# Prompt attention on one core: float32 probabilities as the stationary operand, V as the moving one

## The chip, the cores and the metric

The kernel runs on one core of a Trainium2 chip. The metric is device time in microseconds (us). A run of three timings of the kernel before gave a median of 1132.84 us (1131.6 to 1136.12).

The engines are named as the profile names them: PE (TensorE, matmuls) with PEld (its weight loads: the operand that is loaded is the stationary one, the other streams past it and is the moving one), DVE (VectorE), ACT (ScalarE), POOL (GpSimd) and SP (SyncE, which here only issues DMAs).

## The reference

One decoder layer for a prompt of 1024 tokens and 8 sample tokens: a projection, an attention group (8 heads of 64, 2 key/value heads) with three branches, a recurrent group (HGRN2), and an output stage. The change touches the prompt's attention alone. Cut to that:

```
qg = q / sqrt(64)
# three branches: compressed blocks (c), selected blocks (s), window of 512 (w)
s_x = einsum(qg, k_x) - slope * distance
p_x = softmax(s_x under its mask)
o_x = einsum(p_x, v_x)
o   = g[...,0:1]*o_c + g[...,1:2]*o_s + g[...,2:3]*o_w
```

All of it is float32.

## The kernel before, in words

The program is one static order of instructions for each engine. A scheduler makes that order when the program is built, from the order in which the code is written and from priorities. Each engine then works through its own list in order and waits at semaphores.

The stages follow one another: projection and recurrence, compression of the keys, the projections of the gates, attention, and the output stage (`finish`). The attention stage takes 16 units: 8 blocks of 128 queries times 2 key/value groups, in the order of blocks 5, 6, 7, 4, 3, 2, 1, 0. A unit (`branches`) does branch 2 (compressed keys, one block of at most 63 keys), then branch 0, then branch 1 (blocks of 128 keys each). In all there are 16 blocks of branch 2 and 132 of the other two.

For one block PE makes the scores of four heads at once (keys on partitions, 4 x 128 query columns) with two matmuls into a PSUM tile `ph` (two buffers): `ph<-QA,KA` and `ph<-QB,KB`. ACT takes the exponential into the tile `P` (float32). On some blocks POOL masks `P`. Then `P` is split into two parts that PE can multiply in one pass each (type `fp32r`): `Ph`, a rounded copy, and `Pl`, the rest `P - Ph`. Two blocks in three have the copy on ACT and the subtraction on POOL; every third has both on DVE. V is split ahead of the stage into `Vh` and `Vl`. PE then adds three products into the accumulator `pb` (two buffers), with the 65 columns of V (64 and a column of ones for the denominator) as the stationary operand and the 512 columns of probabilities as the moving one. Branch 2 packs its split parts into one tile `PH` and needs two products (`vcl`, `vch`).

When a branch is done (`output`), ACT copies the accumulator (65 x 512, queries along the free dimension) to `oT`; PE transposes four pieces of it into a tile `pa` (three buffers); DVE computes the factor `rden` (reciprocal of the denominator times the gate) and scales into `og` or `onrm`; POOL adds.

Around this other work is interleaved: `maxima`, which for the unit after next multiplies keys and queries (`pa<-KB,QB`) and takes row maxima on DVE (`junk`, `mx`), then turns them (`pa<-ident,Mp`) into a row of `QB`; and the attention of the 8 sample tokens (`sample_attention`: `sg`, `KT`, `Qr`, `PT`, `two` and others), one step after every second block. The helper `mm` issues all matmuls, so they have one line (L42); `split` has lines L50 and L51.

Of the kernel before, what the change touches and what calls it, by code (L numbers as in the profile page):

```python
# [7 lines left out]
F32 = mybir.dt.float32  # L8
F32R = mybir.dt.float32r
# [4 lines left out]
OP = mybir.AluOpType  # L14
# [6 lines left out]
NB = 8  # L21
# [6 lines left out]
class Kernel:  # L28
# [766 lines left out]
    def prompt_setup(self, ctx):  # L795
        nc, a, ap = self.nc, self.a, self.kvpool
# [11 lines left out]
        for br in range(3):  # L808
            for g in range(2):
                n = self.KA[br, g].shape[1]  # L810
                nc.sync.dma_start(self.KB[br, g][64:68].bitcast(F32), self.kx_d[br, :, :n])
        self.Vh = ap.tile([128, 2, 8, 2, 65], F32R, name="Vh")
        self.Vl = ap.tile([128, 2, 8, 2, 65], F32R, name="Vl")
        self.vch = ap.tile([128, 2, 65], F32R, name="vch")
        self.vcl = ap.tile([64, 2, 65], F32R, name="vcl")
        one = ap.tile([128, 2, 32], F32, name="one")
        for v, val in ((self.Vh, 1.0), (self.Vl, 0.0)):
            nc.gpsimd.memset(one[:, 0 if val else 1], val)
            nc.vector.tensor_copy(v[:, :, :, :, 64], one[:, 0 if val else 1].rearrange("p (a b c) -> p a b c", a=2, b=8))
        nc.vector.tensor_copy(self.vch, one[:, 1, :1, None].to_broadcast([128, 2, 65]))  # L820
        nc.vector.tensor_copy(self.vcl, one[:64, 1, :1, None].to_broadcast([64, 2, 65]))
        nc.vector.tensor_copy(self.vch[:, :, 64], one[:, 0, :2])
        for half in range(2):
            hs = slice(half * 512, half * 512 + 512)
            for br in range(2):
                rows = self.kv_d[1 + br][hs].rearrange("(i p) c -> p i c", p=128)
                k = stage()
                nc.sync.dma_start(k, rows[:, :, :128])
                pt = self.ps_h.tile([128, 512], F32, name="ph")
                for i in range(4):  # L830
                    nc.tensor.transpose(pt[:, i * 128:(i + 1) * 128], k[:, i], self.ident)
                for g in range(2):
                    A, B = self.KA[br, g], self.KB[br, g]
                    src = pt[g * 64:g * 64 + 64]
                    here, there = (A[64:128, hs], B[0:64, hs])[::1 if g else -1]
                    nc.scalar.copy(here, src)
                    nc.sync.dma_start(there.bitcast(F32), here.bitcast(F32))
                    nc.vector.tensor_tensor(A[0:64, hs], src, here.bitcast(F32), op=OP.subtract)
                v = stage()
                nc.sync.dma_start(v, rows[:, :, 128:])  # L840
                sl = (slice(None), br, slice(4 * half, 4 * half + 4), slice(None), slice(0, 64))
                self.split(self.Vh[sl], self.Vl[sl], v.rearrange("p i (h d) -> p i h d", h=2), nc.scalar, nc.gpsimd)

        mask = ap.tile([128, 640], F32, name="mask")
        nc.gpsimd.memset(mask, 0.0)
# [10 lines left out]
        for g in range(2):  # L856
# [3 lines left out]
            nc.scalar.copy(B[0:64, :63], src)  # L860
            nc.scalar.copy(A[64:128, :63], src)
            nc.vector.tensor_tensor(A[0:64, :63], src, (A[64:128, :63] if g else B[0:64, :63]).bitcast(F32), op=OP.subtract)
        vc = self.vcS[:63, NB].rearrange("p (h d) -> p h d", h=2)
        nc.scalar.copy(self.vch[64:127, :, :64], vc)
        self.split(self.vch[:63, :, :64], self.vcl[:63, :, :64], vc, nc.scalar, nc.vector)
        self.zero = ap.tile([128, 4], F32, name="zero")
        nc.gpsimd.memset(self.zero, 0.0)
        self.PH = ap.tile([128, 4, 128], F32R, name="PH")
        self.filled = 64
        self.Mp, self.QB, self.QA, self.nblk = {}, {}, {}, 0  # L870
        for g in range(2):
            for i in range(2):
                Mp = self.Mp[g, i] = ap.tile([128, 4, 4], F32R, name=f"Mp{g}{i}")
# [76 lines left out]
    def branches(self, qb, g, i):  # L950

        nc, wk = self.nc, self.ap
        KA, KB, QA, QB = self.KA, self.KB, self.QA[g, i], self.QB[g, i]
        og = wk.tile([128, 4, 64], F32, name="og", bufs=3)
        for br in (2, 0, 1):
            k0, k1 = (0, 0) if br == 2 else self.ranges(qb)[br]
            acc = self.ps_b.tile([128, 512], F32, name="pb")[:65]
            for kb in range(k0, k1 + 1):
                def block(br=br, kb=kb, first=kb == k0, last=kb == k1, acc=acc):
                    n = 8 * qb + 7 if br == 2 else 128  # L960
                    ks = slice(kb * 128, kb * 128 + n)
                    ps = self.ps_h.tile([128, 512], F32, name="ph")[:n].rearrange("p (h q) -> p h q", q=128)
                    self.mm(ps, KA[br, g][:, ks], QA, True, False)
                    self.mm(ps, KB[br, g][:68, ks], QB, False, True)
                    P = wk.tile([128, 4, 128], F32, name="P", bufs=5)[:n]
                    nc.scalar.activation(P, ps, AF.Exp, scale=0.125)  # L966
                    keep = dict(compare_op=OP.is_ge, fill=0.0)
                    if br == 2:
                        nc.gpsimd.affine_select(P, P, pattern=[[0, 4], [1, 128]], base=qb * 128 - 31, channel_multiplier=-16, **keep)
                    elif kb == qb:  # L970
                        nc.gpsimd.affine_select(P, P, pattern=[[0, 4], [1, 128]], base=0, channel_multiplier=-1, **keep)
                    elif br == 1 and kb == qb - 4:
                        nc.gpsimd.affine_select(P, P, pattern=[[0, 4], [-1, 128]], base=0, channel_multiplier=1, **keep)
                    PH = self.PH if br == 2 else wk.tile([128, 4, 128], F32R, name="Ph", bufs=3)
                    if br == 2:
                        if self.filled > n:
                            nc.vector.tensor_copy(PH, self.zero[:, :, None].to_broadcast([128, 4, 128]))
                        self.filled = n
                    Ph = PH[:n]
                    Pl = PH[64:64 + n] if br == 2 else wk.tile([128, 4, 128], F32R, name="Pl", bufs=2)  # L980
                    self.nblk += 1
                    self.split(Ph, Pl, P, nc.scalar if self.nblk % 3 else nc.vector, nc.gpsimd if self.nblk % 3 else nc.vector)
                    if br == 2:
                        self.mm(acc, self.vcl[:n, g], Ph, True, False)
                        self.mm(acc, self.vch[:, g], PH, False, True)
                    else:
                        vh, vl = self.Vh[:, br, kb, g], self.Vl[:, br, kb, g]
                        self.mm(acc, vh, Ph, first, False)
                        self.mm(acc, vl, Ph, False, False)
                        self.mm(acc, vh, Pl, False, last)  # L990

                yield block

            def output(br=br, acc=acc):
                oT = wk.tile([128, 512], F32, name="oT", bufs=2)[:65]
                nc.scalar.copy(oT, acc)
                pt = self.ps_a.tile([128, 512], F32, name="pa").rearrange("p (h d) -> p h d", h=4)
                for hh in range(4):
                    nc.tensor.transpose(pt[:, hh, :65], oT[:, hh * 128:(hh + 1) * 128], self.ident[:65, :65])
                r = wk.tile([128, 4], F32, name="rden", bufs=2)  # L1000
                nc.vector.tensor_scalar(r, pt[:, :, 64], 1e-30, None, op0=OP.max)
                nc.vector.reciprocal(r, r)
                gi = 12 * g + (0 if br == 2 else 1 + br)
                nc.vector.tensor_tensor(r, r, self.G[:, qb, gi:12 * g + 12:3], op=OP.mult)  # L1004
                rb = r[:, :, None].to_broadcast([128, 4, 64])
                if br == 2:
                    nc.vector.tensor_tensor(og, pt[:, :, :64], rb, op=OP.mult)
                elif qb == 0:
                    for hh in range(4):
                        nc.vector.scalar_tensor_tensor(og[:, hh], pt[:, hh, :64], r[:, hh:hh + 1], og[:, hh], op0=OP.mult, op1=OP.add)  # L1010
                else:
                    t = wk.tile([128, 4, 64], F32, name="onrm", bufs=2)
                    nc.vector.tensor_tensor(t, pt[:, :, :64], rb, op=OP.mult)
                    nc.gpsimd.tensor_tensor(og, og, t, op=OP.add)

            yield output

        def store():
            nc.sync.dma_start(self.oa_d[qb * 128:qb * 128 + 128, g * 256:(g + 1) * 256], og.rearrange("p h d -> p (h d)"))

        yield store
# [397 lines left out]
```

## Time and profile before

| | |
|---|---|
| median of three timings | 1132.84 us |
| the profiled execution's own time | 1139.19 us |
| its span, first to last instruction | 1137.5 us |
| attention stage, read from the timeline | about 549 to 903 us |

The profiled execution is one run, 6.35 us above the median; 1.69 us of it lie outside its span. In the rows below, times are us unless marked ns. PE's busy time counts each matmul from its start to a modelled end, and matmuls overlap, so the step from one start to the next is what a matmul costs PE. The granted clock is the share of PE's full clock: 1.0 is 2.4 GHz, 0.5 is 1.2 GHz.

### The profile page before, as it was taken

The page shows a single profiled execution, that of the slowest core. Times are in us where ns is not written, and L with a number is a line of the kernel's source. Part 1 is how long each engine was busy: PE and PEld are TensorE (multiplying, and loading weights), DVE is VectorE, ACT ScalarE, POOL GpSimd, SP SyncE. Part 2 cuts the span into 40 slices and gives each one's busy share as a digit, 9 for nine tenths or more (in the row PEclk, how much of TensorE's full clock was granted, in tenths as well). Part 3 has the DMA queues.
Part 4 walks back from the last instruction along what each step waited for, and adds up shares of the span by engine and source line. Part 5 has one row for each costly group of instructions (what it writes and reads, how often), then busy time and mean ns, then how long its engine had stood idle before and what let it go on. Part 6 is the DMA issues. An engine that isn't in the chain of part 4 may idle for free.

```text
span 1137.5 us, 18238 instructions
## 1 busy us (share of the span) xinstructions
PE 1061.9 (93%) x6457; PEld 879.9 (77%) x6457; DVE 726.8 (64%) x1931; ACT 465.3 (41%) x939; POOL 391.2 (34%) x378
## 2 busy tenths in 40 slices
PE   4999999999899999999899898898888999999998
PEld 3998799999798998999576565665555688778876
DVE  6857564656655436436686989998999575372213
ACT  4622234223122345422376565656565442141112
POOL 0033233222211130021384665666677333122111
PEclk9999999999899999999798899998799699999999
DMA  6211203434545664215559020005331283131110
GB/s 203 59 32 61 66 13 108 132 103 131 161 145 168 186 211 162 74 61 157 187 163 258 19 56 19 20 19 148 112 94 38 61 244 113 40 102 47 47 42 30
DMA packets 116768, 116.41 MB, mean 102 GB/s; under 512 B 14614, under 2 KB 98926, under 8 KB 114372
## 3 DMA queue, kind: packets, MB, share of 16 engines
q1 hardware_dynamic: 95172, 79.46, 24.2%
q10 hardware_dynamic: 19200, 19.01, 4.9%
q0 software_dynamic: 2304, 16.78, 4.3%
q8 instruction: 51, 0.84, 0.3%
q14 instruction: 41, 0.34, 0.1%
HBM read 84.84 MB, written 29.31 MB: 100 GB/s over the span
## 4 chain that ended last, share of the span: by engine, by line
PE 70%; DVE 15%; DMA 7%; issue 4%; ACT 2%; POOL 1%; SPq 0%; DVEq 0%; ACTq 0%; POOLq 0%
PE pa L42 35%; PE pb L42 20%; PE ph L42 7%; PE pt L42 3%; DMA vb<-v_d 2%; DMA w_raw<-w_in 2%; DVE junk L927 2%; DVE Pl L51 2%; DVE KT L51 1%; PE ph L714 1%; DVE fw_lo L51 1%; DVE rden L1004 1%; DVE Ph L50 1%; DMA sg<-cache_slc_kv,pidx 1%; PE pa L1149 1%
## 5 line engine op out<-in xcount | busy, mean ns | idle before, releaser
L51 POOL TENSOR_TENSOR Pl<-P,Ph 128x512 fp32r<-128x512 f32 x87 | 123.4, 1423 | 59.1 <-PE pb L42 42.5
L42 PE MATMUL pa<-xhi,w_hi 128*128 128x344 f32 x384 | 125.6, 329 | 3.7 <-ACT w_hi L238 2.2
L42 PE MATMUL pa<-xlo,w_hi 128*128 128x344 f32 x384 | 124.1, 325 | 0.0
L42 PE MATMUL pa<-xhi,w_lo 128*128 128x344 f32 x384 | 123.3, 326 | 0.2 <-DVE w_lo L239 0.2
L966 ACT ACTIVATE P<-ph 128x512 f32<-128x512 f32 (+4 forms) x148 | 85.1, 592 | 47.7 <-PE ph L42 44.4
L42 PE MATMUL pa<-KB,QB 65*128 65x320 f32 (+6 forms) x195 | 68.2, 368 | 16.3 <-DVE mx L927 9.9
L927 DVE CUSTOM_DVE_ANT_0 junk<-pa,mask 128x320 bf16<-128x320 f32 (+5 forms) x150 | 72.4, 492 | 13.7 <-PE pa L42 12.5
L42 PE MATMUL pa<-w_lo,xhi 128*128 128x256 f32 (+2 forms) x256 | 79.6, 315 | 0.2 <-DVE w_lo L239 0.2
L238 ACT ACTIVATE w_hi<-w_raw,gpre 128x512 fp32r<-128x512 f32 (+2 forms) x80 | 47.3, 616 | 78.2 <-DMA w_raw<-w_in 45.5
L42 PE MATMUL pa<-w_hi,xlo 128*128 128x256 f32 (+2 forms) x256 | 79.3, 314 | 0.0
L42 PE MATMUL pa<-w_hi,xhi 128*128 128x256 f32 (+2 forms) x256 | 78.5, 316 | 0.0
L42 PEld LDWEIGHTS pa<-xhi,w_hi 128*128 128x128 f32 x384 | 73.3, 191 | 5.3 <-ACT w_hi L238 2.8
L42 PEld LDWEIGHTS pa<-xhi,w_lo 128*128 128x128 f32 x384 | 72.7, 190 | 0.6 <-DVE w_lo L239 0.4
L42 PEld LDWEIGHTS pa<-xlo,w_hi 128*128 128x128 f32 x384 | 73.0, 190 | 0.1
L42 PEld LDWEIGHTS pa<-KB,QB 65*128 65x128 f32 x195 | 39.3, 205 | 37.7 <-DVE mx L927 14.3
L42 PE MATMUL ph<-QA,KA 128*128 128x512 f32 (+4 forms) x148 | 66.2, 448 | 1.6 <-DVE mx L927 1.6
L556 POOL TENSOR_TENSOR K<-K,E 128x512 f32<-128x512 f32 x24 | 34.1, 1423 | 96.9 <-PE pb L42 59.9
L239 DVE SCALAR_TENSOR_TENSOR w_lo<-w_raw,gpre,w_hi 128x512 fp32r<-128x512 f32 (+2 forms) x80 | 52.1, 672 | 23.2 <-ACT w_hi L238 22.4
L42 PE MATMUL pb<-Pl,Vh 128*65 128x512 f32 x132 | 57.6, 436 | 5.5 <-DVE Pl L51 4.2
L42 PE MATMUL pa<-fw_hi,yh 128*128 128x512 f32 (+1 forms) x160 | 61.8, 386 | 0.2 <-ACT fw_hi L50 0.2
L42 PE MATMUL ph<-QB,KB 68*128 68x512 f32 (+4 forms) x148 | 61.3, 431 | 0.4 <-ACT QB L946 0.2
L42 PE MATMUL pa<-fw_hi,yl 128*128 128x512 f32 (+1 forms) x160 | 61.5, 384 | 0.0
(482 smaller groups left out, 2888.1 us busy)
## 6 DMA issues: line engine op xcount, KB each, us to landing
w_raw<-w_in SPq DMA_DIRECT2D x32, 256.0 KB
w_raw<-w_in SPq DMA_DIRECT2D x48, 128.0 KB
VS<-sg SPq DMA_DIRECT2D x8, 512.0 KB
sg<-cache_win_kv SPq DMA_DIRECT2D x16, 256.0 KB
fw_raw<-w_out SPq DMA_DIRECT2D x16, 256.0 KB
fw_raw<-ple_gate SPq DMA_DIRECT2D x16, 256.0 KB
f_x<-x_prompt SPq DMA_DIRECT2D x8, 512.0 KB
win_kv_sample<-cache_win_kv SPq DMA_DIRECT2D x8, 511.0 KB
```

Of the source, the lines that this page charges most:

```text
L42: return self.nc.tensor.matmul(out, lhsT, rhs, start=start, stop=stop, skip_group_check=True)
L50: (hi_eng.copy if hi_eng is self.nc.scalar else hi_eng.tensor_copy)(hi, src)
L51: lo_eng.tensor_tensor(lo, src, hi.bitcast(F32), op=OP.subtract)
L238: nc.scalar.activation(hi, raw, AF.Copy, scale=g)
L239: nc.vector.scalar_tensor_tensor(lo, raw, g, hi.bitcast(F32), op0=OP.mult, op1=OP.subtract)
L556: nc.gpsimd.tensor_tensor(Kv[:, :, 0], Kv[:, :, 0], Ev[:, :, 1:2].to_broadcast([128, nb, m]), op=OP.mult)
L714: nc.tensor.transpose(pt[:, i * 128:(i + 1) * 128], src[b0 + j // 2, kv][:, j % 2, 2 * jp:2 * jp + 2].rearrange("p j d -> p (j d)"), self. ...
L927: nc.vector.tensor_tensor_reduce(junk, pm, mk, 1.0, -1e30, op0=OP.add, op1=OP.max, accum_out=o)
L966: nc.scalar.activation(P, ps, AF.Exp, scale=0.125)
L1004: nc.vector.tensor_tensor(r, r, self.G[:, qb, gi:12 * g + 12:3], op=OP.mult)
L1149: nc.tensor.transpose(pt[:, j * 128:(j + 1) * 128], rows(j), self.ident)
```

## The change

The splits go. `P` itself, float32, is the stationary operand: for each head 128 key rows by 128 query columns. V, float32 too and not split, is the moving one with its 65 columns. One matmul in the code for each head and block adds into the accumulator, whose four heads now lie side by side with queries on partitions. So nothing is transposed when a branch is done: DVE reads the accumulator, keeps the denominator's reciprocal in a free column of it, and scales from it. V is loaded with 16 DMAs straight into its tile, where 4 DMAs and 4 splits stood.

```diff
-        self.Vh = ap.tile([128, 2, 8, 2, 65], F32R, name="Vh")
-        self.Vl = ap.tile([128, 2, 8, 2, 65], F32R, name="Vl")
...
+        self.V = ap.tile([128, 2, 8, 2, 65], F32, name="V32")
+        self.vc = ap.tile([64, 2, 65], F32, name="vc32")
+        nc.gpsimd.memset(self.V[:, :, :, :, 64], 1.0)
+        nc.gpsimd.memset(self.vc[:, :, 64], 1.0)
...
-                v = stage()
-                nc.sync.dma_start(v, rows[:, :, 128:])
-                sl = (slice(None), br, slice(4 * half, 4 * half + 4), slice(None), slice(0, 64))
-                self.split(self.Vh[sl], self.Vl[sl], v.rearrange("p i (h d) -> p i h d", h=2), nc.scalar, nc.gpsimd)
+                for i in range(4 * half, 4 * half + 4):
+                    nc.sync.dma_start(self.V[:, br, i, :, :64], self.kv_d[1 + br][i * 128:i * 128 + 128, 128:].rearrange("p (h d) -> p h d", h=2))
...
-            acc = self.ps_b.tile([128, 512], F32, name="pb")[:65]
+            acc = self.ps_b.tile([128, 512], F32, name="pb").rearrange("p (h d) -> p h d", h=4)
...
-                    self.split(Ph, Pl, P, nc.scalar if self.nblk % 3 else nc.vector, nc.gpsimd if self.nblk % 3 else nc.vector)
-                    if br == 2:
-                        self.mm(acc, self.vcl[:n, g], Ph, True, False)
-                        self.mm(acc, self.vch[:, g], PH, False, True)
-                    else:
-                        vh, vl = self.Vh[:, br, kb, g], self.Vl[:, br, kb, g]
-                        self.mm(acc, vh, Ph, first, False)
-                        self.mm(acc, vl, Ph, False, False)
-                        self.mm(acc, vh, Pl, False, last)
+                    v = self.vc[:n, g] if br == 2 else self.V[:, br, kb, g]
+                    for hh in range(4):
+                        m = self.mm(acc[:, hh, :65], P[:, hh], v, first and hh == 0, last)
...
             def output(br=br, acc=acc):
-                oT = wk.tile([128, 512], F32, name="oT", bufs=2)[:65]
-                nc.scalar.copy(oT, acc)
-                pt = self.ps_a.tile([128, 512], F32, name="pa").rearrange("p (h d) -> p h d", h=4)
-                for hh in range(4):
-                    nc.tensor.transpose(pt[:, hh, :65], oT[:, hh * 128:(hh + 1) * 128], self.ident[:65, :65])
+                pt = acc
...
+                nc.vector.tensor_scalar(pt[:, :, 66], pt[:, :, 64], 1e-30, None, op0=OP.max)
+                nc.vector.reciprocal(pt[:, :, 66], pt[:, :, 66])
+                nc.vector.tensor_tensor(r, pt[:, :, 66], self.G[:, qb, gi:12 * g + 12:3], op=OP.mult)
```

On PE, in branch 1 of the first unit, this stood in the order before (a row is line, operation, out<-in, shape of what is written, and a count where a row repeats; `sg` belongs to the sample tokens):

```order
L42 MATMUL pb<-Ph,Vh 65x512
L42 MATMUL pb<-Ph,Vl 65x512
L42 MATMUL pa<-KB_5360,QB_5494 128x448
L1149 MATMUL pa<-ident,sg 128x128 x4
L42 MATMUL pb<-Pl,Vh 65x512
L42 MATMUL ph<-QA,KA_5363 128x512
L42 MATMUL ph<-QB_5487,KB_5364 128x512
```

And this stands there now, two blocks further on in the same branch:

```order
L42 MATMUL pb<-V_5375,P 128x65 x3
L1121 MATMUL pa<-ident,sg 128x128 x8
L42 MATMUL pa<-KB_5360,QB_5481 128x448
L42 MATMUL pb<-V_5375,P 128x65
L42 MATMUL ph<-QA,KA_5363 128x512
L42 MATMUL ph<-QB_5474,KB_5364 128x512
L42 MATMUL pb<-V_5375,P 128x65 x4
```

The three wide products of a block have become four narrow ones, one for each head, and other work is set between them as before. At the entry to the stage, 7 products of `maxima` stood between the last matmul of the gate projection and the first scores; now 16 do.

On DVE, where the first branch of the first unit is put out, this stood before (L1001 to L1007 are the output; the rows around it are a split and the maxima):

```order
L1001 TENSOR_SCALAR rden<-pa 128x4
L1002 RECIPROCAL rden<-rden 128x4
L50 CAST Ph<-P 128x512
L1004 TENSOR_TENSOR rden<-rden,G 128x4
L1007 TENSOR_TENSOR og<-pa,rden 128x256
```

And this stands at the end of the first unit now, where two branches are put out at once (`KT` belongs to the sample tokens, L912 to the maxima, L974 to L985 are the output):

```order
L51 TENSOR_TENSOR KT_6383<-pa,KT_6382 128x512
L912 ISA junk,mx<-pa,mask 128x320
L912 ISA mx 128x1
L974 TENSOR_SCALAR pb<-pb 128x4 x2
L975 RECIPROCAL pb<-pb 128x4 x2
L976 TENSOR_TENSOR rden<-pb,G 128x4 x2
L985 TENSOR_TENSOR onrm<-pb,rden 128x256
```

DVE no longer splits, and its output reads `pb` itself, the accumulator, where it read a copy that PE had turned.

On ACT, in the first unit, this stood before:

```order
L50 CAST Ph<-P 128x512 x2
L966 ACTIVATE P<-ph 128x512 x2
L50 CAST Ph<-P 128x512
L50 CAST KT_6265<-pa 128x512
L996 COPY oT<-pb 65x512
```

And this stands there now:

```order
L951 ACTIVATE P<-ph 128x512 x2
L50 CAST KT_6238<-pa 128x512
L1152 COPY K_6196<-pa 128x512
L951 ACTIVATE P<-ph 128x512 x4
L50 CAST KT_6289<-pa 128x512
```

The copies into `Ph` and `oT` are gone; the exponentials follow one another more closely.

## Rows read from the trace of the kernel before

**Rows 1.** The page, part 1: busy us, share of the span, instructions.
```profile
PE 1061.9 (93%) x6457; PEld 879.9 (77%) x6457; DVE 726.8 (64%) x1931; ACT 465.3 (41%) x939; POOL 391.2 (34%) x378
```

**Rows 2.** Busy PE, PEld, DVE, ACT, POOL; clock, DMA, GB/s, by stretch.
```profile
549.00:903.00 354.00, 312.27 (x1570) 205.70 (x1571) 308.17 (x903) 216.72 (x398) 224.98 (x217) 0.89 0.32 92
...
650.00:700.00 50.00, 46.26 (x229) 31.47 (x228) 45.81 (x129) 31.39 (x61) 30.37 (x28) 0.98 0.15 40
```

**Rows 3.** The chain that ended last, in the attention stage: shares by line.
```profile
by line: PE pb L42 16.3%; PE ph L42 11.8%; issue 8.7%; PE pa L42 6.3%; DVE junk L927 5.7%; PE pt L42 5.1%; DVE Pl L51 5.1%; DVE KT L51 4.5%; DVE rden L1004 4.1%; DVE Ph L50 3.5%; DVE fw_lo L51 3.3%; DMA sg<-cache_slc_kv,pidx 3.2%; PE pa L11
```

**Rows 4.** PE's groups in the attention stage: shapes, count, busy, mean ns, idle before.
```profile
L42 PE MATMUL ph<-QA,KA 128*128 128x512 f32 (+4 forms) x148 | 66.2, 448 | 1.6 <-DVE mx L927 1.6
L42 PE MATMUL pa<-KB,QB 65*128 65x320 f32 (+6 forms) x176 | 62.3, 371 | 16.3 <-DVE mx L927 9.9 <-DVE mx L929 2.3 <-DVE rden L1002 1.0
...
L42 PE MATMUL pb<-Pl,Vh 128*65 128x512 f32 x131 | 57.2, 437 | 5.5 <-DVE Pl L51 4.2 <-POOL Pl L51 0.7 <-DVE rden L1004 0.3
...
L999 PE MATMUL pa<-ident,oT 65*128 65x65 f32 x184 | 22.4, 237 | 0.6 <-DVE mx L927 0.5
...
L42 PE MATMUL pt<-KT,PT 128*16 128x128 f32 x192 | 16.8, 230 | 1.1 <-DVE KT L51 1.1
```

**Rows 5.** Timeline of PE where it is packed: start, duration, what.
```profile
653.83 0.34 PE L42 MATMUL pa<-KB,QB 65*128 65x384 f32 x1
654.00 0.39 PE L42 MATMUL pb<-Pl,Vh 128*65 128x512 f32 x1
654.23 0.39 PE L42 MATMUL pb<-Ph,Vh 128*65 128x512 f32 x1
...
660.44 0.41 PE L999 MATMUL pa<-ident,oT 65*128 65x65 f32 x4
660.65 0.42 PE L42 MATMUL pa<-KB,QB 65*128 65x384 f32 x1
```

**Rows 6.** The tile `two`: count, least/median/most ns, first and last start, shape.
```profile
L42 PE MATMUL pt<-two,o x16: 251/251/272, 765.0 to 766.7; 16*128 16x8 f32 x16
```

**Rows 7.** Timeline of PE in the compression: float32 products with 63 stationary columns.
```profile
450.42 0.90 PE L42 MATMUL pt<-w,w1r 128*63 128x64 f32 x12
451.25 0.45 PE L42 MATMUL pb<-x,w1h 128*128 128x384 f32 x1
```

**Rows 8.** Groups of DVE, ACT and POOL in the attention stage.
```profile
L51 DVE TENSOR_TENSOR Pl<-P,Ph 128x512 fp32r<-128x512 f32 x45 | 39.9, 887 | 2.4 <-PE pb L42 2.1
L50 DVE CAST Ph<-P 128x512 fp32r<-128x512 f32 x45 | 34.7, 771 | 3.5 <-ACT P L966 1.9 <-PE pb L42 1.0 <-POOL P L971 0.7
L1004 DVE TENSOR_TENSOR rden<-rden,G 128x4 f32<-128x4 f32 x46 | 29.0, 630 | 0.5
...
L1013 DVE TENSOR_TENSOR onrm<-pa,rden 128x256 f32<-128x256 f32 x28 | 11.7, 419 | 0.4
...
L50 ACT CAST Ph<-P 128x512 fp32r<-128x512 f32 x87 | 53.2, 618 | 11.3 <-POOL Pl L51 3.8 <-PE pb L42 2.7 <-POOL P L971 2.1
L996 ACT COPY oT<-pb 65x512 f32<-65x512 f32 x47 | 27.1, 579 | 20.4 <-PE pb L42 16.1 <-PE pa L999 3.9
...
L51 POOL TENSOR_TENSOR Pl<-P,Ph 128x512 fp32r<-128x512 f32 x87 | 123.4, 1423 | 59.1 <-PE pb L42 42.5 <-ACT Ph L50 14.9 <-ACT P L966 1.0
...
L51 POOL TENSOR_TENSOR PH<-P,PH 47x512 fp32r<-47x512 f32 (+7 forms) x12 | 16.1, 1339 | 9.0 <-ACT PH L50 7.4 <-issue 1.3
```

**Rows 9.** The line L1004: least, median and most ns over the kernel.
```profile
L1004 DVE TENSOR_TENSOR rden<-rden,G x48: 147/560/1862, 574.8 to 910.5; 128x4 f32<-128x4 f32 x48
```

**Rows 10.** Timeline of DVE at the entry to the stage: the maxima's steps.
```profile
550.10 0.48 DVE L927 CUSTOM_DVE_ANT_0 junk<-pa,mask 128x320 bf16<-128x320 f32 x1
550.51 0.08 DVE L927 DVE_READ_ACCUMULATOR2_ANT mx<- 128x1 f32 x1
```

**Rows 11.** Timeline of SP (DMA issues) while keys and V are loaded.
```profile
500.52 0.50 SPq L828 DMA_DIRECT2D st<-kv_d  x1
505.92 0.36 SPq L840 DMA_DIRECT2D st<-kv_d  x1
```

More of the change, by code (lines that the diff above doesn't have):

```diff
@@ L811, in prompt_setup @@
                 nc.sync.dma_start(self.KB[br, g][64:68].bitcast(F32), self.kx_d[br, :, :n])
-        self.Vh = ap.tile([128, 2, 8, 2, 65], F32R, name="Vh")
-        self.Vl = ap.tile([128, 2, 8, 2, 65], F32R, name="Vl")
[L814 to L822, printed above, removed]
+        self.V = ap.tile([128, 2, 8, 2, 65], F32, name="V32")
+        self.vc = ap.tile([64, 2, 65], F32, name="vc32")
+        nc.gpsimd.memset(self.V[:, :, :, :, 64], 1.0)
+        nc.gpsimd.memset(self.vc[:, :, 64], 1.0)
         for half in range(2):
@@ L862, in prompt_setup @@
             nc.vector.tensor_tensor(A[0:64, :63], src, (A[64:128, :63] if g else B[0:64, :63]).bitcast(F32), op=OP.subtract)
[L863 to L870, printed above, removed]
+        nc.vector.tensor_copy(self.vc[:63, :, :64], self.vcS[:63, NB].rearrange("p (h d) -> p h d", h=2))
+        self.Mp, self.QB, self.QA = {}, {}, {}
         for g in range(2):
@@ L973, in block @@
                         nc.gpsimd.affine_select(P, P, pattern=[[0, 4], [-1, 128]], base=0, channel_multiplier=1, **keep)
-                    PH = self.PH if br == 2 else wk.tile([128, 4, 128], F32R, name="Ph", bufs=3)
-                    if br == 2:
[L976 to L980, printed above, removed]
@@ L981, in block @@
-                    self.nblk += 1
-                    self.split(Ph, Pl, P, nc.scalar if self.nblk % 3 else nc.vector, nc.gpsimd if self.nblk % 3 else nc.vector)
-                    if br == 2:
-                        self.mm(acc, self.vcl[:n, g], Ph, True, False)
-                        self.mm(acc, self.vch[:, g], PH, False, True)
-                    else:
-                        vh, vl = self.Vh[:, br, kb, g], self.Vl[:, br, kb, g]
-                        self.mm(acc, vh, Ph, first, False)
-                        self.mm(acc, vl, Ph, False, False)
-                        self.mm(acc, vh, Pl, False, last)
+                    v = self.vc[:n, g] if br == 2 else self.V[:, br, kb, g]
@@ L992, in branches @@
+                    for hh in range(4):
+                        m = self.mm(acc[:, hh, :65], P[:, hh], v, first and hh == 0, last)
+                        if first:
+                            if hh:
+                                self.after(m, start)
+                            else:
+                                start = m
                 yield block
             def output(br=br, acc=acc):
-                oT = wk.tile([128, 512], F32, name="oT", bufs=2)[:65]
-                nc.scalar.copy(oT, acc)
@@ L997, in output @@
-                pt = self.ps_a.tile([128, 512], F32, name="pa").rearrange("p (h d) -> p h d", h=4)
-                for hh in range(4):
-                    nc.tensor.transpose(pt[:, hh, :65], oT[:, hh * 128:(hh + 1) * 128], self.ident[:65, :65])
+                pt = acc
                 r = wk.tile([128, 4], F32, name="rden", bufs=2)
-                nc.vector.tensor_scalar(r, pt[:, :, 64], 1e-30, None, op0=OP.max)
-                nc.vector.reciprocal(r, r)
                 gi = 12 * g + (0 if br == 2 else 1 + br)
-                nc.vector.tensor_tensor(r, r, self.G[:, qb, gi:12 * g + 12:3], op=OP.mult)
+                nc.vector.tensor_scalar(pt[:, :, 66], pt[:, :, 64], 1e-30, None, op0=OP.max)
```

## The prediction

> **What bounds the kernel now.** I read the page's first part first. PE is busy 93% of the span and DVE 64% [rows 1]; that is an average over stages, and only the attention stage is changed. So I read the busy time by stretch there: of 354 us PE is busy 312, DVE 308, POOL 225, ACT 217, at a mean granted clock of 0.89 [rows 2]. Two engines look full. The reader should mistrust PE's figure, since a matmul's modelled time overlaps the next one's. The step from start to start is what it costs: in a packed piece of the timeline 0.23 us for 512 columns (654.00 to 654.23), 0.17 for 384, and 0.05 for each of the four transposes of an output (the next product starts 0.21 us after the first of them) [rows 5].
>
> With these steps PE's own work in the stage can be counted at the full clock. 148 blocks have two score products, 132 blocks three products with V, 16 blocks (branch 2) two, and the sample tokens have 48 of the same width: 772 products of 512 columns at 0.23 us, 178 us. Add 176 products of the maxima at about 0.16 us, 28 us, and some 530 small ones, of which 184 turn outputs and 192 are the sample tokens' [rows 4], at 0.05 to 0.1 us, 35 us. That is about 240 us of 354. The other 114 us are waits and stretches at 1.2 GHz; a mean clock of 0.89 over 354 us alone stands for up to 39 us.
>
> The chain of waits says on whom PE waits. It runs in turn over PE (the four lines shown sum to 39.5%) and DVE: the maxima's line L927 5.7%, the split's `Pl` 5.1% and `Ph` 3.5%, `rden` 4.1%, `KT` 4.5% [rows 3]. So the stage is bound by two engines that hand work to each other, both with little slack.
>
> **What the change costs on PE.** Before, a block of branches 0 and 1 cost three steps of 0.23, 0.69 us. Now it has four float32 products, each with 128 stationary columns and 65 moving ones. The trace of before has no such product, but it has close neighbours. The records show that a float32 product is two records: the code makes 8 products into `two`'s output and the trace has 16 [rows 6]. Those have 128 stationary columns and only 8 moving ones, and yet 15 steps take 1.7 us, 0.113 us each [rows 6], so it is not the moving columns that set the pace there. Products with 63 stationary and 64 moving columns take at most 0.069 us a record (0.83 us for 12) [rows 7]. The lower bound for a new product is therefore 2 x 0.069, the upper one 2 x 0.113 = 0.226 us. I take the upper one, since its stationary operand has the same 128 columns. Four make 0.90 us a block.
>
> The Trainium skill bears on this from two sides. "FP8 and Floating Point Precision", TensorE Precision Notes, says that true FP32 takes four passes through the array; by that alone a head would cost 4 x 65 columns, and the product with V would get cheaper. "TensorE: Matmul & The Clock Gate", LDWEIGHTS (loading the stationary operand), gives a load as the stationary columns divided by 1.2, in ns, which is 107 for 128 columns; that speaks against this change, and the 0.113 us of the neighbour agree with it, while the transposes' 0.05 us, with 128 stationary columns too, do not.
>
> The sum for PE at the full clock: added 148 x 0.90 = 134 us; gone 396 x 0.23 = 91 us, 32 x 0.23 = 7 us for branch 2, and 192 transposes x 0.05 = 10 us. PE's work rises by 26 us, from 240 to 266 (with the lower bound it would fall by 26: 148 x 8 x 0.069 = 82).
>
> **What it takes away.** On DVE every third split: 39.9 + 34.7 us [rows 8], and some 8 us of clearing and splitting `PH`. On ACT 53 us of `Ph` and 27 us of `oT`; on POOL 123 + 16 us, more than half of its 225 [rows 2, 8]. A third effect: DVE's `rden` writes four numbers a partition and takes 630 ns on average but 147 at best [rows 8, 9], so it is held up while it runs, and so are splits that take 887 ns. I read that as DVE and POOL getting in each other's way; with 62% of POOL's work gone I expect 62% of the excess to go: 46 x 0.48 x 0.62 = 14 us of DVE's time. DVE comes down from 308 us to about 210. "SBUF — State Buffer", Who interferes with whom, says that a DVE instruction with two SBUF inputs contends with POOL's reads; the 147 to 1862 ns of that one shape agree.
>
> What of it lies on the path is read from the chain, 1% being 3.5 us. `Pl` 18 us and `Ph` 12 us go whole. Of `rden`'s 14.5 us, 77% is above its best, and 62% of that goes: 7 us. `KT`, 16 us, loses perhaps a fifth, 3 us. For `PH`, POOL's `Pl` and the copies, too short to stand among the chain's first entries, I put 4 us. Together 44 us. Against that stand PE's 26 us: if all of it falls on the path the stage gains 18 us, if only PE's share of 40% does, 34 us. Nothing says which; I take 26. Waits that go also save clock: the clock is 0.98 where PE is packed and 0.89 on average [rows 2]. The lower level costs PE's work about 39 x 240/354 = 27 us; I put a quarter, 7 us.
>
> **The entry to the stage.** SP issues 12 more DMAs (16 loads of V for 4), at 0.36 to 0.50 us each [rows 11], 5 us of its queue, ahead of the loads of queries. But V no longer takes staging buffers: SP stood still from 501.0 to 505.9 us between two such loads [rows 11], and with V's loads out of the rotation I expect that wait to shrink. I cost SP at nothing net, 5 us at worst. In the order 16 products of the maxima, not 7, now follow the gate projection. They are DVE's time, 0.41 us a step [rows 10], that PE's projection no longer covers: 9 x 0.41 = 4 us on the path.
>
> **The new wait.** The accumulator was free as soon as ACT had copied it. Now it is held until DVE has done its four output steps, three of them on four numbers a partition, 0.15 us each if they take what `rden` takes at best [rows 9], and 0.42 for the scaling [rows 8], 0.9 us; and DVE's list has other work ahead of them: `KT`, which itself waits for ACT and PE, and the maxima. Behind the waiting product on PE stand the next scores and maxima, for which ACT and DVE wait. There are two accumulators and 48 outputs. I cost it at nothing, since the transposes made PE and DVE wait on each other before too (ACT's copies waited 3.9 us on L999, PE's maxima 1.0 on `rden` [rows 4, 8]), and take its price as a rival.
>
> **The forecast.** -26 - 7 + 4 = -29 us. The profiled execution would go from 1139 to 1110 us; the median of three lies 6.35 us lower, and 1132.84 - 29 = 1104 us.
>
> **The rivals.**
> 1. *The accumulator's wait eats the gain.* Place: PE before the first product of a branch; price: if each of the 32 outputs of branches 0 and 1 holds PE for 1.5 us (DVE's four steps and one row ahead of them), 48 us; at 0.9 us each it cancels the forecast's 29. For it: an output with two branches at once, behind `KT`. Against: PE's list has scores and maxima between. Time 1104 + 48 = 1152 at full price; I give this and any state where DVE's waits simply return elsewhere 0.14, with times from 1139 to 1152.
> 2. *The loads hide.* If float32 loads of 128 columns cost what 63 do, PE's work falls by 26 instead of rising by 26. By the share on the path (40% to all) that is 21 to 52 us more: 1052 to 1083. The four-pass rule above says this; the row of `two` speaks against it. Chance 0.06.
> 3. *PE is packed throughout.* DVE at 210 of some 300 us never holds it: 266 us of work and 15 of waits and clock, against 354: -73 + 4, 1064 us. For it: 650 to 700 us is nearly so today, at a clock of 0.98. Chance 0.08.
> 4. *The clock falls.* The stretch of `two` (765.0 to 766.7) is the only one of such products, too short to tell. If the stage ran at 1.2 GHz half of the time instead of the 22% that 0.89 stands for, 266 us of work would cost 0.28 x 266 = 74 us more, 1178. Packed stretches held 0.98. Chance 0.05.
> 5. *Nothing to measure.* Gain and price cancel, 1127 to 1138: 0.09.
>
> The forecast's own case, 1083 to 1127, has 0.58.
>
> **How the numbers follow.** About 0.5%, 5.7 us, is what a measurement of this kernel can tell from no change. Faster: the forecast, rivals 2 and 3, 0.58 + 0.06 + 0.08, 0.72. Same 0.09. Slower: rivals 1 and 4, 0.19. The range for 8 in 10: from 1068, which leaves out half of rivals 2 and 3 (0.07), to 1143, which leaves out rival 4 and half of rival 1 (0.12).
>
> **What would show it.** In the profile after: steps of 0.11 us between records of `pb<-V32,P`, eight a block (right), or 0.06 (rival 2). No `Ph`, `Pl`, `oT`. DVE near 210 us and POOL near 85 in the stage, `rden` well under 630 ns. A stage of about 326 us, by the scores' first and last start. A long wait of `pb` on DVE's output lines would show rival 1, a stage clock well below 0.89 rival 4. The prediction is wrong if PE's step is not 0.11, if waits on DVE do not shrink, or if the stages outside move by more than 5 us.

## The result and the profile after

The changed kernel is slower: 1178.8 us median against 1132.22 us in the same series, a ratio of 1.0405 with a 95% interval from 1.033 to 1.048. The ratio leaves out the one of the four executions, 1201.32 us, that lies over 1.5% above the fastest. Forecast were 1104 us. The time equals, by luck to the us, what the forecast gave for its rival 4, to which it allowed a chance of 0.05.

The page of the profile after, parts 1 and 2 (busy us, share of the span, instructions; then the granted clock in 40 slices of 29 us):

```profile
PE 1141.7 (97%) x7021; PEld 1018.7 (87%) x7021; DVE 617.9 (53%) x1822; ACT 389.5 (33%) x786; POOL 239.4 (20%) x274
PEclk9999999999899999997899969955555599999999
```

PE is busy 97% of the span (before 93% [rows 1]), DVE and POOL are relieved. The row of the clock shows six slices in a row at 5 tenths, 1.2 GHz, and shallower dips ahead of them. By stretch (columns as in [rows 2]; the third figure from the end is the granted clock):

```profile
549.00:949.00 400.00, 398.25 (x2168) 349.27 (x2169) 197.75 (x816) 144.44 (x255) 70.31 (x107) 0.72 0.28 80
570.50:672.00 101.50, 100.97 (x699) 89.22 (x698) 58.69 (x205) 50.27 (x91) 24.33 (x34) 1.00 0.50 141
673.00:696.00 23.00, 23.00 (x101) 21.39 (x100) 8.85 (x37) 6.50 (x13) 1.97 (x3) 0.50 0.00 1
697.00:761.00 64.00, 64.00 (x548) 56.27 (x546) 39.13 (x149) 30.48 (x53) 9.40 (x16) 1.00 0.10 28
761.50:942.00 180.50, 180.50 (x703) 158.86 (x702) 71.59 (x336) 48.16 (x83) 32.89 (x51) 0.50 0.23 67
943.00:960.00 17.00, 17.00 (x84) 14.16 (x83) 7.67 (x25) 4.48 (x10) 0.00 (x0) 1.00 0.57 180
```

The stage now lasts 400 us to the last output's step (948.1 us; before 910.5 [rows 9], so 38 us longer, as is the span: 1175.5 us against 1137.5). PE is busy 398 of 400 us. But for 180 us it is busy at 1.2 GHz without a break, and nothing else is short of time: DVE works 72 of these 180 us, POOL 33, the DMA engines 23%. Of the waits 3 us are left (engine and line, waited for: us, times, longest), where before the maxima alone held PE for 9.9 us [rows 4]:

```profile
PE ph L42 <- DVE mx L912: 1.7, 1, 1.7
PE pa L42 <- DVE mx L912: 0.5, 1, 0.5
PE pt L42 <- DVE pr L1028: 0.5, 2, 0.3
PE pa L42 <- DVE Mp L919: 0.3, 1, 0.3
```

The timeline of PE at both clocks (start, duration, what):

```profile
605.85 1.89 PE L42 MATMUL pb<-V,P 128*128 128x65 f32 x16
607.55 0.48 PE L42 MATMUL pt<-KT,Qr 128*128 128x512 f32 x1
...
755.90 1.23 PE L42 MATMUL pb<-V,P 128*128 128x65 f32 x10
757.06 1.95 PE L42 MATMUL pt<-two,o 16*128 16x8 f32 x16
758.93 0.50 PE L42 MATMUL ph<-QA,KA 128*128 128x512 f32 x1
...
939.61 1.80 PE L42 MATMUL pb<-V,P 128*128 128x65 f32 x8
941.20 1.03 PE L1268 MATMUL ph<-ident,f_oa 128*128 128x128 f32 x4
941.91 0.55 PE L42 MATMUL pa<-fw_hi,yl 128*128 128x512 f32 x1
942.30 0.40 PE L42 MATMUL pa<-fw_hi,yh 128*128 128x512 f32 x1
942.53 0.40 PE L42 MATMUL pa<-fw_lo,yh 128*128 128x512 f32 x1
```

At the full clock 16 records of the new product take 1.70 us, until the next product starts (605.85 to 607.55), 0.11 each. At 1.2 GHz eight take 1.59 us (939.61 to 941.20), 0.20 each. The clock comes back at 942, just as the 512-column products of the output stage begin to follow one another. It had gone at 761, shortly behind a series of short products (`two`, 8 columns, 757.06) between records of V.

Groups of the stage (shapes, count, busy, mean ns, idle before):

```profile
L42 PE MATMUL pb<-V,P 128*128 128x65 f32 x1052 | 186.7, 328 | 0.0
...
L51 DVE TENSOR_TENSOR KT<-VS,KT 128x512 fp32r<-128x512 f32 x16 | 11.4, 710 | 0.1
...
L51 DVE TENSOR_TENSOR fw_lo<-fw_raw,fw_hi 128x512 fp32r<-128x512 f32 x16 | 10.8, 687 | 3.3 <-ACT fw_hi L50 3.3
...
L976 DVE TENSOR_TENSOR rden<-pb,G 128x4 f32<-128x4 f32 x47 | 7.3, 158 | 0.8
```

`rden` is down from 630 ns to 158 [rows 8], but it is not the same step: before, both its operands lay in SBUF (`rden` and `G`), now one is the accumulator `pb` in PSUM. DVE is down from 308 us to 198, POOL from 225 to 70 [rows 2].

### The profile page after: what moved, and what is told of

Its sections match the earlier page's. It is cut to its first block, busy times and chain, and to the rows that moved or that the text cites. A ratio compares the mean times of both kernels' runs of the same rounds, so it can differ in the third digit from the quotient of the medians.

```text
span 1175.5 us, 18909 instructions
## 1 busy us (share of the span) xinstructions
PE 1141.7 (97%) x7021; PEld 1018.7 (87%) x7021; DVE 617.9 (53%) x1822; ACT 389.5 (33%) x786; POOL 239.4 (20%) x274
## 4 chain that ended last, share of the span: by engine, by line
PE 89%; DMA 5%; DVE 3%; ACT 1%; issue 1%; POOL 0%; SPq 0%; ACTq 0%; DVEq 0%; POOLq 0%
PE pa L42 39%; PE pb L42 31%; PE ph L42 12%; PE pt L42 3%; DMA vb<-v_d 2%; DMA w_raw<-w_in 2%; PE ph L714 1%; PE pa L1121 1%; DMA V<-x_prompt 1%; PE ph L1315 1%; DVE junk L912 0%; PE ph L1268 0%; DVE w_lo L239 0%; PE ph L218 0%; PE pt L609 0%
## 5 line engine op out<-in xcount | busy, mean ns | idle before, releaser
L42 PEld LDWEIGHTS pb<-V,P 128*128 128x128 f32 x1056 | 195.6, 255 | 15.9 <-issue 1.6
L42 PE MATMUL pb<-V,P 128*128 128x65 f32 x1056 | 187.1, 328 | 0.0
L912 DVE CUSTOM_DVE_ANT_0 junk<-pa,mask 128x320 bf16<-128x320 f32 (+5 forms) x150 | 73.7, 497 | 57.9 <-PE pa L42 56.8
L42 PE MATMUL ph<-QA,KA 128*128 128x512 f32 (+4 forms) x148 | 82.8, 561 | 0.2
L42 PE MATMUL pa<-KB,QB 65*128 65x320 f32 (+6 forms) x195 | 80.8, 450 | 1.5 <-DVE mx L912 0.7
L42 PE MATMUL ph<-QB,KB 68*128 68x512 f32 (+4 forms) x148 | 73.6, 507 | 0.0
L42 PE MATMUL pa<-fw_lo,yh 128*128 128x512 f32 (+1 forms) x160 | 61.8, 386 | 0.0
L42 PE MATMUL pb<-x,w1h 128*128 128x384 f32 (+1 forms) x192 | 55.9, 353 | 1.6 <-ACT x L50 1.6
```

Source lines behind the costliest of these rows:

```text
L42: return self.nc.tensor.matmul(out, lhsT, rhs, start=start, stop=stop, skip_group_check=True)
L912: nc.vector.tensor_tensor_reduce(junk, pm, mk, 1.0, -1e30, op0=OP.add, op1=OP.max, accum_out=o)
```

## The experiments

**Theory A**: the narrow products, packed one behind the other, leave TensorE at 1.2 GHz, and this costs more than the whole change brings. **Rival B**: the low clock comes with the float32 form, its loads, or an engine that is packed, whatever streams. **Rival C**: the clock is a by-product, and the added 26 us of PE's work with some wait explain the 47 us by which the kernel is slower.

### 128 moving columns

V's rows hold both groups, 130 columns in one piece. The product streams 128 of them, of which 65 are read:

```diff
-                    v = self.vc[:n, g] if br == 2 else self.V[:, br, kb, g]
+                    v = (self.vc[:n] if br == 2 else self.V[:, br, kb]).rearrange("p a b -> p (a b)")
+                    v = v[:, 130 - 128:] if g else v[:, :128]
...
-                        m = self.mm(acc[:, hh, :65], P[:, hh], v, first and hh == 0, last)
+                        m = self.mm(acc[:, hh, :128], P[:, hh], v, first and hh == 0, last)
...
-                pt = acc
+                pt, sc = (acc[:, :, 128 - 65:], acc[:, :, 0]) if g else (acc, acc[:, :, 66])
```

> The products P by V take as moving operand the 128 columns of V that hold both groups' values (the own 65 among them) in place of 65; the loads, the number of products and everything else stay. Theory A (the narrow products keep TensorE at 1.2 GHz although it is packed): a record still takes the 0.11 us that the load sets, the granted clock of the stage (0.75 or so after the change, 1.2 GHz unbroken from 761 to 942 us) rises above 0.9, and the time falls by 50 to 80 us to 1100 to 1130 us. Rival B (the low clock comes with the float32 form, its loads, or the packed engine as such, whatever streams): the clock stays as it is, the time is 1175 to 1190 us. Rival C (the clock is a by-product and the 26 us of added work and a wait explain the 45 us): 1175 to 1190 us with a higher clock.

Measured: 1096.41 us median, ratio to before 0.968 (0.960 to 0.976): the fastest kernel of this study, ahead of both. The page's clock row:

```profile
PEclk9999999999999999999969999999999999999999
```

The stretch of the stage to its last output, and a piece of PE's timeline:

```profile
549.00:868.00 319.00, 311.74 (x2174) 270.78 (x2175) 200.30 (x823) 144.28 (x255) 73.21 (x114) 0.96 0.37 104
```
```profile
618.87 2.40 PE L42 MATMUL pb<-V,P 128*128 128x128 f32 x20
621.02 0.94 PE L42 MATMUL pt<-KT,Qr 128*128 128x512 f32 x3
```

Nearly twice as many columns cost no time: 20 records take 2.15 us (618.87 to 621.02), 0.11 each, as with 65. The same loads, the same number of products and the same float32 form now run at 0.96. Rival B falls with that, and rival C with the time: the added products are still there, and 82 us are gone.

### 96 and 80 moving columns

The same edit with 96 and 80 for 128.

> As the run with 128 moving columns, with 96. Theory A: between the changed kernel and the 128-column one, 1115 to 1165 us, with a stretch at 1.2 GHz shorter than 181 us; if it acts as a switch, at one of the two ends. Rivals B and C: 1175 to 1190 us.

> As the runs with 128 and 96 moving columns, with 80. Theory A (narrow products leave the engine at 1.2 GHz) by degrees: between the 1178.8 us of 65 columns and the 1103 us of 96, some 1130 to 1160 us, low stretches in all shorter than with 65 and longer than with 96. Theory A as a switch with its point below 80 columns: 1095 to 1110 us; with its point above: 1170 to 1185 us. Without theory A (the 96- and 128-column runs fast for another reason, as the place of the results in the accumulator): 1095 to 1110 us.

Measured: 96 columns 1102.96 us, 0.972 (0.964 to 0.980); 80 columns 1180.48 us, 1.043 (1.037 to 1.049). The clock rows of the two pages, 96 first (its profiled execution, 1120.27 us, was the longest of its four):

```profile
PEclk9999999999999899999879996996699999999999
```
```profile
PEclk9999999999999999998599999975555599999999
```

The longest low stretch of each, 96 first:

```profile
766.00:803.00 37.00, 37.00 (x141) 32.48 (x141) 16.77 (x64) 9.38 (x17) 8.74 (x12) 0.50 0.46 135
```
```profile
779.50:946.00 166.50, 157.84 (x606) 137.57 (x607) 62.42 (x291) 42.77 (x74) 28.68 (x45) 0.50 0.21 61
```

Both lose the clock in the same part of the program, at 766 and 779 us, as the changed kernel does at 761; the 128-column kernel does too, at 755, for 3 us. With 96 columns it is back after 37 us, with 80 only where the stage ends. So in these traces the width does not decide whether the clock falls there but how soon it comes back. The mean clock over the span, on record for every execution, says the same of those without a trace: 0.982 to 0.986 in the four with 128 columns, 0.955 to 0.981 with 96, 0.896 to 0.909 with 80, 0.879 to 0.903 in the eight with 65. "By degrees" was wrong: 80 columns lie near 65 (1180.48 us against 1178.8, and against 1194.89 in a repeat in the same series), and 96 lie 78 us below them. Since the layout of the accumulator and the reading of the outputs are the same with 80, 96 and 128, these are not the cause either.

### One product twice, and the same work in packs

The first kernel does each block's first product of scores twice over the same output, 148 products more. The second does it eight times more, but only in the 16 compressed blocks, 128 products more; the added work, 31 and 27 us at 0.21 us each, is nearly the same.

```diff
                     self.mm(ps, KA[br, g][:, ks], QA, True, False)
+                    self.mm(ps, KA[br, g][:, ks], QA, True, False)
```
```diff
+                    for _ in range(8 if br == 2 else 0):
+                        self.mm(ps, KA[br, g][:, ks], QA, True, False)
                     self.mm(ps, KA[br, g][:, ks], QA, True, False)
```

> The changed kernel with each block's first product of scores done twice (512 columns, same output, the second time over the first): 132 products of 0.21 us at 2.4 GHz added, 28 us of pure extra work. Theory A: the clock of the stage rises, and gives back as much as the work costs or more: 1130 to 1185 us. Rivals B and C: the work is added at the clock of before, 1205 to 1225 us.

> The same extra work as in the run that did one product of scores twice in each block (about 130 wide products, 28 us at 2.4 GHz), but in 16 packs of eight, one ahead of each compressed-branch block, over the same output. If the low clock, once there, lasts until a stretch of wide products comes: a pack ends it, low stretches are shorter than the distance of two packs (some 20 us), time 1140 to 1190 us. If it is the share of narrow products over the whole stage that decides: as the run with the work spread out, 1136 to 1236 us, low stretches of over 100 us that run through packs.

Measured, spread out: 1235.87, 1209.05, 1136.27 and 1212.88 us, too far apart for a ratio. In packs: 1143.98 us, 1.011 (1.005 to 1.016), with all four times within 3 us. That is 35 us less than the changed kernel's 1178.8, and 51 less than its repeat in the same series (1194.89, below), with 27 us of work more. The long low stretch of the kernel with the work spread out:

```profile
782.50:1000.00 217.50, 217.50 (x805) 187.72 (x806) 75.32 (x343) 49.97 (x86) 34.91 (x53) 0.50 0.21 60
```

The stretches of the kernel with packs, and a piece of its PE timeline:

```profile
674.50:701.00 26.50, 26.50 (x113) 24.50 (x112) 10.07 (x43) 7.27 (x14) 1.99 (x3) 0.50 0.00 1
797.00:820.50 23.50, 23.27 (x85) 19.70 (x86) 11.16 (x44) 8.19 (x15) 3.46 (x6) 0.50 0.29 84
821.50:858.00 36.50, 35.76 (x248) 30.39 (x247) 20.23 (x118) 14.63 (x26) 9.04 (x15) 1.00 0.23 66
858.50:871.50 13.00, 13.00 (x51) 10.99 (x51) 2.24 (x16) 1.79 (x3) 1.33 (x2) 0.50 0.12 31
```
```profile
818.55 1.52 PE L42 MATMUL ph<-QA,KA 128*31 128x512 f32 x3
819.87 0.52 PE L42 MATMUL pb<-V,P 128*128 128x65 f32 x2
820.15 0.67 PE L42 MATMUL ph<-QA,KA 128*31 128x512 f32 x1
820.61 0.40 PE L42 MATMUL pb<-V,P 128*128 128x65 f32 x2
820.82 0.42 PE L42 MATMUL ph<-QA,KA 128*31 128x512 f32 x1
821.08 0.33 PE L42 MATMUL pb<-V,P 128*128 128x65 f32 x2
```

In packs no low stretch of the traced execution is longer than 28 us. The one from 797 us ends at 820.6 us, in the middle of a pack (`ph<-QA,KA` with 31 keys; from 820.15 to the next product it is 0.46 us, from 820.82 it is 0.26), the one from 858 at 872, at the end of another. The one from 674 ends at 701 with no pack near, as in the changed kernel at 696, where 16 products of the sample tokens (`KT,PT`) stand between scores and maxima. Spread out, the same work did not end the stretch in the traced execution (217 us at 0.50 with PE always busy); theory A as I had put it, an average over the stage, missed that. What the traces show is narrower: the low clock, once there, lasted through the narrow stream, and in the kernel with packs it came back twice while wide products stood close together. That the packs brought it back is what the two times and traces speak for; what the chip goes by, they do not show. One execution of the spread-out form, 1136 us, stayed mostly at the full clock: its mean over the span is 0.968, where the other three have 0.882 to 0.902. Why that one differs stays open.

### The changed kernel once more

> The changed kernel as it is, once more, beside the others. If the low stretch is set by the program alone, it lies where it lay, 761 to 942 us, with the two short ones at 546 and 672 us. If it depends on the history of the execution, its ends move, and the span moves with the time spent low: half of each us more at 1.2 GHz. Time 1165 to 1200 us.

Measured: 1194.89 us, 1.054 (1.046 to 1.061); the two intervals of this kernel touch. The longest low stretch:

```profile
786.00:970.00 184.00, 184.00 (x714) 161.97 (x715) 73.06 (x344) 48.76 (x84) 32.96 (x51) 0.50 0.24 69
```

The last stretch has the length it had (184 us; 181 before) and starts 25 us later; the shorter ones ahead of it, at 550, 683 and 755 us, add up to 96 us in place of 48: the time of this kernel depends on how long it stays low, and so it spreads (1174 to 1205 us over all its runs, where the kernel before has 1125 to 1140).

### Half of the change: V stationary, no splits

```diff
-                    for hh in range(4):
-                        m = self.mm(acc[:, hh, :65], P[:, hh], v, first and hh == 0, last)
...
+                    self.mm(acc, v, P, first, last)
...
+                oT = wk.tile([128, 512], F32, name="oT", bufs=2)[:65]
+                nc.scalar.copy(oT, acc)
...
+                    nc.tensor.transpose(pt[:, hh, :65], oT[:, hh * 128:(hh + 1) * 128], self.ident[:65, :65])
```

> Half of the change: float32 probabilities without splits, but V stationary and the probabilities moving as before, 512 columns in one product (four passes), with the copy and the four transposes of each output back. Per block about 0.85 us in place of 0.90 at full clock, 48 outputs with some 0.3 us of transposes each come back: the same 266 us of work within a few us. Theory A: clock of the stage above 0.9, 1095 to 1130 us. Rival B, if it is the float32 form or the packed engine: 1175 to 1195 us; if it is the loads, as theory A, and the 128-column run decides.

Measured: 1124.02 us, 0.992 (0.988 to 0.996).

The stage to its last output, and a piece of PE's timeline:

```profile
549.00:890.00 341.00, 331.13 (x1457) 184.41 (x1455) 202.51 (x824) 168.80 (x302) 76.95 (x119) 0.91 0.34 96
```
```profile
719.76 1.88 PE L42 MATMUL pb<-P,V 128*65 128x512 f32 x4
721.48 0.41 PE L969 MATMUL pa<-ident,oT 65*128 65x65 f32 x4
```

Four records of 512 columns take 1.72 us until the next product starts, 0.43 each; a block has two, 0.86 us: the price of the 128-column form, to which the transposes come. The clock, 0.91, is far from 0.72 and no better than before. So float32 without splits alone is worth 7 us. Of the 28 us between it and the 128-column form, by estimate from these figures, some 18 are clock (0.09 x 341 = 31 us lost against 13) and about 10 the 192 transposes, at 0.05 us each [rows 5]. The Trainium skill, "FP8 and Floating Point Precision", TensorE Precision Notes, counts four passes through the array for true FP32. This trace comes near it: a product's two records take 0.86 us, and four times the 0.23 us that a split product of 512 columns takes [rows 5] is 0.92.

Scaled from 512 columns to fewer, the 0.43 us of a record would be 0.05 with 65 columns and 0.11 with 128, by estimate. Measured are 0.11 with both. So with 65 the columns do not set the pace; with 128 they would just begin to.

### A mixture

The 128-column form for the compressed and the window branch, for the 72 blocks of the selected branch the products of the kernel before:

```diff
+                    if br == 0:
...
+                        self.mm(pb[:65], vh, Ph, first, False)
+                        self.mm(pb[:65], vl, Ph, False, False)
+                        self.mm(pb[:65], vh, Pl, False, last)
+                        return
```

> A candidate: the 128-column form for the compressed and the window branch, the split form of the kernel before (three products of 512 columns, copy and transposes of the output) for the 72 blocks of the selected branch. TensorE has 72 times about 0.26 us less of products and 16 outputs with some 0.4 us of transposes more, 12 us less in all; VectorE, idle for over 40% of the stage in the 128-column run, takes a third of 72 splits. If TensorE alone is the bound there: 1080 to 1092 us; if the splits bring waits for VectorE and POOL back: 1095 to 1110 us.

Measured: 1113.6 us, 0.983 (0.977 to 0.989), slower than the 128-column form throughout.

The stage to its last output, and the groups of the splits on POOL and DVE:

```profile
549.00:877.00 328.00, 313.13 (x1852) 240.21 (x1853) 238.17 (x857) 178.42 (x320) 137.13 (x157) 0.92 0.35 99
```
```profile
L51 POOL TENSOR_TENSOR Pl<-P,Ph 128x512 fp32r<-128x512 f32 x48 | 64.0, 1338 | 50.8 <-ACT Ph L50 32.0 <-PE pb L42 10.4 <-DVE sm L1086 4.9
...
L50 DVE CAST Ph<-P 128x512 fp32r<-128x512 f32 x24 | 20.7, 863 | 3.4 <-PE pb L42 2.9 <-POOL Pl L51 0.4
L51 DVE TENSOR_TENSOR Pl<-P,Ph 128x512 fp32r<-128x512 f32 x24 | 20.1, 836 | 1.4 <-PE pb L42 0.8
```

PE stands still for 15 of 328 us in place of 7 of 319, and the clock is 0.92 in place of 0.96 (26 us lost to it against 13). The splits cost POOL 64 us and DVE 41 again. That these waits are also what lowers the clock is argued from the two moving together, not shown.

## Why the prediction was wrong

**The new product's price: right.** Forecast 0.113 us a record, from the row of `two`; measured 0.11. The columns do not set the pace (128 columns: the same); with 0.069 us for 63 stationary columns [rows 7] this fits the load. Only where records of a compressed block alternate with V's in pairs do they take longer, 0.18 us (`vc`, two in 669.23 to 669.60 us of the changed kernel; rows at the end of this part).

**What it takes away: the sums right within 15 us, one of them for another reason.** DVE 198 us (forecast 210), POOL 70 (85), ACT 144 (137). That POOL holds up DVE is borne out by steps which the change doesn't touch and which read two operands in SBUF: `KT<-VS,KT` and `fw_lo` fell from 975 and 1158 ns to 710 and 687. `rden` does not bear it out. It fell to 158 ns, close to its best, where 62% of the excess was forecast to go with POOL's work; but the change also moved one of its operands to PSUM. The mixture tells the two apart: there POOL still works 137 us, and a step that reads SBUF twice is still slow, while `rden` is as short as with 70.

```profile
L51 DVE TENSOR_TENSOR KT<-VS,KT 128x512 fp32r<-128x512 f32 x16 | 15.6, 975 | 0.0
L51 DVE TENSOR_TENSOR KT<-pa,KT 128x512 fp32r<-128x512 f32 x16 | 11.0, 685 | 4.0 <-ACT KT L50 4.0
...
L51 DVE TENSOR_TENSOR KT<-VS,KT 128x512 fp32r<-128x512 f32 x16 | 12.9, 805 | 0.9 <-ACT KT L50 0.9
L999 DVE TENSOR_TENSOR rden<-pb,G 128x4 f32<-128x4 f32 x31 | 4.7, 152 | 0.1
```

The first two rows are from the kernel before (549 to 903 us), the last two from the mixture (549 to 877). `KT<-pa,KT`, with one operand in PSUM, was at 685 ns before, too. So `rden` fell because of where it reads, and the prediction did not see that.

**The accumulator's wait, costed at nothing: right.** PE's list of waits has no row of `pb` on an output's step, in the 128-column kernel, whose clock stayed up, as little as in the changed one; rival 1 did not happen. Rivals 2 and 5 fell with the record's 0.11 us and the stage's length, 38 us more where 28 less were forecast. Rival 3's condition came true, PE is packed throughout (398 of 400 us), but not its gain.

**The entry: right in the net.** The first score starts at 553.0, 2.9 us later than before; forecast +4. But the gate projection ends at 541.3 us, 6.4 earlier, over the 5 us that the prediction named as a sign against it, and the piece from there to the first score grew by 9.2 us, not 4.

**The step that failed: "Waits that go also save clock", -7 us.** It rested on the clock being 0.98 where PE is packed [rows 2]. That stretch was packed mainly with wide products: of its 229 records (650 to 700 us), 165 stream 320 to 512 columns. The changed kernel is packed with 65 columns, and its clock is 0.72 over 400 us, a loss of 0.28 x 400 = 112 us. Before, 0.90 over the 362 us to the last output lost 36. The clock costs 76 us more, where 7 less were forecast. Beside that the stage gains 76 - 38 = 38 us, against the forecast's 22 without its clock term; part of that is no gain, since a slow PE hides waits for others, and a record at 1.2 GHz took 0.20 us, not twice 0.11. The 128-column kernel, the same but for the width, has a stage 81 us shorter, where the two clocks differ by 112 - 13 = 99 us.

The fair test of the other terms is the 128-column kernel, whose clock stayed up: its stage ends 43 us earlier than before (867.0 against 910.5), of which 36 - 0.04 x 319 = 23 us are clock, and 20 are the rest, against 22. Its 1096 us stand 8 us from the forecast. So the sum came out right but for the clock, and the sign of the result hung on that. Not every part of it was right: with 7 us of waits and 13 of clock the 128-column stage leaves 299 of 319 us to PE's work, where 266 were counted, and before it was 284 (362 less 42 and 36), where 240 were counted. By this estimate the count of steps is 33 to 44 us short on both sides, the "114 us" of waits and low clock before were nearer to 80, and the difference of the two, 15 where 26 were forecast, hides most of the error.

**The rival that came true**, 4, named the right cause at the wrong chance, and its price was luck. It multiplies a share of the time (0.28) by work at the full clock; 266 us of work take 266/0.75 = 355 us with half of the time at 1.2 GHz and 266/0.89 = 299 with the old share, 56 us more and not 74, which makes 1160. The stage's 0.72 stands for 56% of the time. The row of `two`, 1.7 us long, could not speak for or against, and I let the packed rows of another kind of product decide.

**Open:** what starts a low stretch. In every kernel here one starts at the entry (546 to 554 us) and one near the short products around `two` (753 to 782 us), before too (553 and 768 us, but back within 17 and 7 us; six more of 3 to 21 us lie in its stage). In the changed kernel, its repeat, the 96 columns and the two kernels with extra products a third starts at 672 to 693 us, behind records of compressed blocks that alternate with V's; with 80 and 128 columns none does there:

```profile
669.23 0.43 PE L42 MATMUL pb<-vc,P 63*128 63x65 f32 x2
669.60 0.66 PE L42 MATMUL pb<-V,P 128*128 128x65 f32 x4
```

A kernel without these pieces was not tried.

## What to carry to other kernels

A busy TensorE is not a fast one: where a change puts narrow products in place of wide ones, forecast the granted clock as a term of its own, and read it afterwards by stretch before looking for a wait. Where the load of the stationary operand sets the pace, widen the moving operand up to what the load covers, even with columns that nobody reads: here 63 spare columns turned 4% slower into 3% faster, and 31 did nearly as much, but 15 did nothing of the kind. And a low clock can last long after it began, in a stream that ran at the full one shortly before; look at what ended it as well as at what stood ahead of it.

## What the runs showed of the hardware

- TensorE, busy without a gap, stayed at 1.2 GHz for 181, 184 and 217 us in a stream that had run at 2.4 GHz for 100 us shortly before (570.5 to 672 us, clock 1.00, in the changed kernel).
- Adding 27 us of wide products in packs made the changed kernel 35 us faster, 51 against its repeat.
- A float32 product with 128 stationary columns took the same 0.11 us a record with 65 and with 128 moving columns.
- DVE's 128 x 512 step with two operands in SBUF (`KT<-VS,KT`) took 975 ns with POOL busy 225 us of the stage, 805 with 137 and 710 with 70; the one with an operand in PSUM (`KT<-pa,KT`) took 685 to 690 ns each time.
- DVE's 128 x 4 step took 630 ns on average with two operands in SBUF, and 152 to 158 with one of them in PSUM, with POOL busy 137 us as with 70.
